# Unused pads in the SBUF pools of a one-core hybrid decoder layer: other starting bytes for weight and moving tiles

## The chip, the cores and the metric

The kernel runs on one core of one Trainium2 chip. The metric is the device time of one execution in microseconds. Before the change it was 1142.21 us, the median of 3 runs (1141.86 to 1142.72).

## What is computed

One decoder layer on 512 tokens of width 1024, in float32. Cut to its products:

```python
h = x
h = h + 0.5 * swiglu(rmsnorm(h), ffn1_w_gate, ffn1_w_up, ffn1_w_down)     # width 2816
u, v, z, xbc, dt = split(rmsnorm(h) @ w_in)
ya = rmsnorm(spatial_gating(gelu(u), layernorm(gelu(v))))                  # 8 heads, chunks of 128
yb = mamba2_mixer(z, xbc, dt)                                              # chunked scan, 16 heads
h = h + concatenate([ya, yb]) @ w_out
h = h + 0.5 * swiglu(rmsnorm(h), ffn2_w_gate, ffn2_w_up, ffn2_w_down)
h = h + sigmoid(rmsnorm(h) @ ple_w_gate + ple_b_gate) * (p @ ple_w_proj)
return rmsnorm(h)
```

## The kernel before

All activations lie with features on the 128 partitions and the 512 tokens along the free dimension. Every large product is done in three passes over float32r parts: a float32 matrix is split into a high part (a cast on ScalarE) and a low part (the rest, a subtraction on VectorE), and TensorE adds high x high, high x low and low x high. `passes` (lines 192 to 196) does this for most products, with 512 moving columns per matmul: the down projections of both FFNs, the input and output projections of the mixer, the final gate. The last three tiles of that gate run in halves of 256 columns.

The up and gate projections of the two FFNs go through `Group.product` (lines 499 to 513), which uses a seven-product scheme over 2 x 2 blocks with 256 moving columns per matmul; line 510 issues these. Here the stationary operand is a 128 x 128 piece of a weight part and the moving one is a piece of an activation form.

The order of work is written out by hand: `run` (line 328) walks a list of steps, loading six steps ahead, splitting two steps ahead, and recording the order of TensorE, VectorE, ScalarE and SyncE as written.

The names that matter here:

- `raw`, `rawb`, `raw0`, `rawd`, `s1`: weights as loaded, 128 x 1024. `whi`, `wlo` and, in the FFNs, for every fourth weight unit `whix`, `wlox`: their parts. TensorE takes 128-column pieces of them as stationary operand.
- `xfa`, `xfb`: activation forms of the FFNs, the moving operands of line 510.
- `ghi`, `glo`: the gated hidden activations, the moving operands of the down projections. `ya`, `yb`: outputs of the two mixers, moving operands of the output projection.
- `x`: normed activations for the input projections and the gate, moving operand there. In one product (the v part, lines 1053 to 1058) the roles are exchanged: `x` is stationary and the weights `whi`, `wlo` move.

SBUF tiles come from three pools. `base` (named `sb`) holds what lives through the program, among it `raw`, `whi` and `wlo`. Two further regions, one growing from the left behind `base` and one that ends at the top of SBUF, are released and opened again between stages: `ffn1_left`, `mix_left`, `ffn2_left` and `ple_left`, `ffn1_right`, `mix_right`, `ffn2_right` and `ple_right`. `REGION` (line 53) says which tile lies where. `open_region` (lines 85 to 89) releases the pool of a side and opens the next:

```python
def open_region(side, name):
    if region[side] is not None:
        region[side].release()
    names[side] = name
    region[side] = tc.alloc_tile_pool(name=name, bufs=1, side=side, reuse_waits="tile")
```

Within a pool, tiles lie one behind the other in the order of their tags. Pieces that TensorE takes from a tile begin 512 bytes, or a multiple of that, behind the tile's start, so a piece begins at the same byte of a 512-byte line as its tile.

Of the kernel before, what the change touches and what calls it, by code (L numbers as in the profile page):

```python
# [22 lines left out]
F32 = mybir.dt.float32  # L23
# [4 lines left out]
P = 128  # L28
# [24 lines left out]
REGION = dict.fromkeys(("raw0", "D1", "X12", "F", "xfa", "xfb", "x", "xs", "u", "emb"), "left") | dict.fromkeys(  # L53
    ("rawb", "whix", "wlox", "s1", "rawd", "ghi", "glo", "g", "u2", "p7", "ya", "yb", "convin", "o"), "right",
)
HEADS = 16
HD = 64
GROUPS = 2
# [18 lines left out]
def layer_kernel(ctx: ExitStack, tc: tile.TileContext, a: dict, out: bass.AP):  # L77
    nc = tc.nc
    PSUM = bass.MemoryType.PSUM
    base = ctx.enter_context(tc.tile_pool(name="sb", bufs=1))  # L80

    region = {"left": None, "right": None}
    names = {}

    def open_region(side, name):
        if region[side] is not None:
            region[side].release()
        names[side] = name
        region[side] = tc.alloc_tile_pool(name=name, bufs=1, side=side, reuse_waits="tile")

    psum = ctx.enter_context(tc.tile_pool(name="ps", bufs=1, space=PSUM))
    dram = ctx.enter_context(tc.tile_pool(name="dr", bufs=1, space=bass.MemoryType.DRAM))
    count = [0]

    def sb(tag, shape=(P, T), dt=F32):
        count[0] += 1
        pool = region[REGION[tag]] if tag in REGION else base
        return pool.tile(list(shape), dt, tag=tag, bufs=BUFS.get(tag, 1), name=f"{tag}_{count[0]}")

    open_region("left", "ffn1_left")  # L100
    open_region("right", "ffn1_right")

    def bank(tag, n):
# [13 lines left out]
    def tmp():  # L117
        return sb("tmp")
# [209 lines left out]
    def run(steps, opened=None):  # L328
# [11 lines left out]
        for i in range(-3, n + 2):  # L340
            if 0 <= i < n - LOADS:
                ahead = i + LOADS
                if opened is not None and i <= opened < ahead and steps[ahead].from_right:
                    held.append(ahead)
                else:
                    do(ahead, "load")
            do(i, "product")
            if i == opened:
                open_region("right", "ffn2_right")
                for k in held:  # L350
                    do(k, "load")
            late = 0 <= i - 1 < n and not steps[i - 1].urgent
            if 0 <= i - 2 < n and len(steps[i - 2].after) > 1:
                steps[i - 2].after[1]()
            for what in ("split", "after") if late else ("after", "split"):
                if what == "split":
                    do(i + 2, "split")
                    do(i + 3, "sums")
                elif 0 <= i - 1 < n and steps[i - 1].after:
                    steps[i - 1].after[0]()  # L360
                if what == "after":
                    do(i, "rest")
# [364 lines left out]
        return Step(product, load, None, split, (out,), True)  # L727

    h = [sb("h") for _ in range(ND)]
    norm = Norm(nc.vector)  # L730
    x_ffn1, x_mix = [], []
    ffn1 = former("ffn1_norm", x_ffn1)
# [32 lines left out]
    def project(unit, w=None):  # L765
# [4 lines left out]

    small = lambda tag: sb(tag, (P, HEADS * NC))

# [4 lines left out]
    nc.vector.tensor_tensor(  # L777
        both[:, :, HEADS : 2 * HEADS],
        w_dt.raw.rearrange("p (k m) -> p k m", k=ND)[:, :, :HEADS],
        both[:, :, :HEADS].bitcast(F32), ALU.subtract,  # L780
    )
# [6 lines left out]
    dt_raw = tmp()  # L788
    nc.vector.tensor_copy(dt_raw[: 2 * HEADS], ps[: 2 * HEADS])

# [24 lines left out]
    for c in range(NC):  # L815
        nc.tensor.transpose(
            dt_ps[:, 2 * c * HEADS : 2 * (c + 1) * HEADS],
            dt_raw[: 2 * HEADS, c * P : (c + 1) * P], ident[: 2 * HEADS, : 2 * HEADS],
# [464 lines left out]
    rows_out(halves[0], r_a)  # L1283
    rows_out(halves[1], factors(halves[1], sq_b))
    for side in region:
        region[side].release()


def _laid_out(i):
# [87 lines left out]
```

## Time and profile before

| | |
|---|---|
| median of 3 runs | 1142.21 us |
| the profiled execution | 1142.69 us |
| its span, first to last instruction | 1141.0 us |
| granted TensorE clock, mean | 0.988 |
| TensorE, matmuls | 1104.4 us busy, 6778 records |
| TensorE, weight loads | 978.6 us busy, 6778 records |
| VectorE / ScalarE / GpSimd | 827.0 / 515.6 / 156.0 us busy |
| moved by DMA | 154.34 MB, 135 GB/s over the span |

In the rows of the profile PE is TensorE with its matmuls, PEld its weight loads, DVE VectorE, ACT ScalarE and POOL GpSimd. A row of groups reads: line, engine, operation, output <- inputs, rows and columns of the array, output shape, count | busy us, mean ns of one | idle us before them and what ended it. A buffer's number is left out of its name, and of two inputs of a matmul the first named is not always the moving one. Matmuls overlap: one starts well before the last has ended, and the ends are modelled. A row of windows reads: stretch, its length, busy us and (count) of the engine, granted clock, DMA share, GB/s.

### The profile page before, as it was taken

The numbers are of one execution on the slowest core, as the hardware profiler recorded it, in microseconds if no ns is written. First come the engines' busy times: TensorE is split into PE (matmuls) and PEld (weight loads), VectorE is DVE, ScalarE is ACT, GpSimd is POOL, SyncE is SP. The second block draws the span as 40 slices with busy tenths as digits, with TensorE's granted clock in tenths as the row PEclk, the third lists the DMA queues.
The fourth block names the chain that finished last, engine by engine and source line by source line (L and its number), as shares of the span: only waits on it lengthen the run. The fifth ranks groups of instructions, "written<-read, shape, count | busy, mean of one in ns | idle before, by whom it ended". The sixth has DMA issues, their size and how long they took to land. (4 is left out here: it accounts for less than half of the span.)

```text
span 1141.0 us, 16731 instructions
## 1 busy us (share of the span) xinstructions
PE 1104.4 (97%) x6778; PEld 978.6 (86%) x6778; DVE 827.0 (72%) x1088; ACT 515.6 (45%) x680; POOL 156.0 (14%) x138
## 2 busy tenths in 40 slices
PE   6899999999999999999999999989999999999997
PEld 5889999999998788777778877888999999999886
DVE  6787767676777687798775564878777677776855
ACT  5644443444344465423543343544434434344555
POOL 1000000000000301476421100000000000000211
PEclk8899999999999999999999999999999999999998
DMA  9566556555621322353422223586666555542512
GB/s 343 140 185 180 159 161 165 136 138 153 185 92 57 93 82 87 98 170 120 130 74 92 76 91 111 139 212 166 167 167 166 153 151 160 144 115 75 166 38 74
DMA packets 46861, 154.34 MB, mean 135 GB/s; under 512 B 5312, under 2 KB 5568, under 8 KB 46784
## 3 DMA queue, kind: packets, MB, share of 16 engines
q1 hardware_dynamic: 34128, 117.98, 31.0%
q0 software_dynamic: 6912, 25.17, 12.5%
q10 hardware_dynamic: 5744, 10.12, 2.8%
q8 instruction: 53, 0.87, 0.3%
q14 instruction: 24, 0.20, 0.1%
HBM read 148.99 MB, written 4.26 MB: 134 GB/s over the span
## 5 line engine op out<-in xcount | busy, mean ns | idle before, releaser
L510 PE MATMUL mm<-xfb,whi 128*128 128x256 f32 x800 | 145.8, 283 | 3.0 <-ACT acc L575 1.9
L510 PEld LDWEIGHTS mm<-xfb,whi 128*128 128x128 f32 x800 | 125.1, 190 | 4.7 <-ACT acc L575 2.1
L510 PE MATMUL mm<-xfb,wlo 128*128 128x256 f32 x400 | 113.2, 283 | 0.1
L397 DVE TENSOR_TENSOR wlo<-raw,whi 128x1024 fp32r<-128x1024 f32 x69 | 84.4, 1223 | 35.9 <-ACT whi L396 35.6
L196 PE MATMUL sm<-ghi,wlo 128*128 128x512 f32 x268 | 105.8, 395 | 0.7 <-DVE wlo L397 0.7
L195 PE MATMUL sm<-glo,whi 128*128 128x512 f32 x268 | 105.1, 392 | 0.1
L194 PE MATMUL sm<-ghi,whi 128*128 128x512 f32 x268 | 104.5, 390 | 0.0
L510 PE MATMUL acc<-xfb,whi 128*128 128x256 f32 x528 | 96.5, 283 | 0.7 <-DVE g L594 0.7
L596 ACT ACTIVATE g<-g 128x512 f32<-128x512 f32 x44 | 27.8, 632 | 143.4 <-DVE g L595 143.4
L396 ACT CAST whi<-raw 128x1024 fp32r<-128x1024 f32 x69 | 71.8, 1046 | 41.0 <-DVE raw L520 16.0
L510 PEld LDWEIGHTS acc<-xfb,whi 128*128 128x128 f32 x528 | 82.8, 190 | 2.2 <-issue 0.9
L510 PE MATMUL acc<-xfb,wlo 128*128 128x256 f32 x264 | 75.0, 284 | 1.5 <-DVE wlo L397 1.5
L510 PEld LDWEIGHTS mm<-xfb,wlo 128*128 128x128 f32 x400 | 76.0, 190 | 0.3 <-DVE wlo L397 0.3
L397 DVE TENSOR_TENSOR wlo<-rawd,whi 128x1024 fp32r<-128x1024 f32 (+1 forms) x37 | 41.5, 1121 | 44.5 <-ACT whi L396 44.4
L525 POOL DMA_DIRECT2D raw<-in_ffn_gu x22 | 18.8, 856 | 395.1 <-DMA raw<-in_ffn_gu 119.2
L649 DVE SCALAR_TENSOR_TENSOR h<-sm,h 128x512 f32<-128x512 f32 x96 | 63.3, 684 | 11.5 <-PE sm L196 11.5
L397 DVE TENSOR_TENSOR wlo<-rawb,whi 128x1024 fp32r<-128x1024 f32 x48 | 58.7, 1224 | 16.7 <-ACT whi L396 16.7
L164 ACT CAST whi<-raw 128x1024 fp32r<-128x1024 f32 x44 | 45.8, 1043 | 48.5 <-issue 14.8
L165 DVE TENSOR_TENSOR wlo<-raw,whi 128x1024 fp32r<-128x1024 f32 x44 | 57.9, 1317 | 12.8 <-ACT whi L164 12.6
L237 POOL TENSOR_TENSOR ssum<-ssum,tmp 128x512 f32<-128x512 f32 x27 | 38.3, 1419 | 207.4 <-ACT tmp L236 206.9
L194 PE MATMUL mm<-x,whi 128*128 128x512 f32 x160 | 64.3, 402 | 0.0
L196 PE MATMUL mm<-x,wlo 128*128 128x512 f32 x160 | 63.4, 396 | 0.0
(332 smaller groups left out, 2969.6 us busy)
## 6 DMA issues: line engine op xcount, KB each, us to landing
raw<-in_ffn_gu SPq DMA_DIRECT2D x56, 512.0 KB, 4.5
rawd<-in_ffn_down SPq DMA_DIRECT2D x40, 512.0 KB, 3.8
rawb<-in_ffn_gu SPq DMA_DIRECT2D x32, 512.0 KB, 4.9
raw<-in_w_in SPq DMA_DIRECT2D x29, 512.0 KB, 3.6
s<-in_ffn_gu SPq DMA_DIRECT2D x22, 512.0 KB, 4.6
raw<-in_ffn_gu POOLq DMA_DIRECT2D x22, 512.0 KB, 5.5
s<-in_ffn_gu POOLq DMA_DIRECT2D x22, 512.0 KB, 7.3
raw<-in_w_out SPq DMA_DIRECT2D x16, 512.0 KB, 3.5
```

Source lines behind the costliest of these rows:

```text
L164: nc.scalar.copy(self.hi[:, c], self.raw[:, c])
L165: nc.vector.tensor_tensor(self.lo[:, c], self.raw[:, c], self.hi[:, c].bitcast(F32), ALU.subtract)
L194: nc.tensor.matmul(ps, whi, xhi, start=first, stop=False)
L195: nc.tensor.matmul(ps, whi, xlo, start=False, stop=False)
L196: nc.tensor.matmul(ps, wlo, xhi, start=False, stop=last)
L237: self.engines[i].tensor_tensor(self.totals[i], self.totals[i], sq, ALU.add)
L396: nc.scalar.copy(self.hi[:, :n], raw[:, :n])
L397: nc.vector.tensor_tensor(self.lo[:, :n], raw[:, :n], self.hi[:, :n].bitcast(F32), ALU.subtract)
L510: nc.tensor.matmul(o, wt[:, c], xt, start=fresh and p == m == n == 0, stop=last and n == 2, skip_group_check=True,)
L525: nc.gpsimd.dma_start(w21.raw, self.src[0], accum_op=ALU.add)
L596: nc.scalar.activation(t, t, AF.Silu)
L649: nc.vector.scalar_tensor_tensor(h[d], ps[d], 0.5, h[d], ALU.mult, ALU.add)
```

## The change

An unused tile of a chosen size, a pad, is put into the pools: 480 bytes per partition into `base` right behind `h`, 480 bytes at the start of `ffn1_left` and `ffn2_left`, 32 bytes at the start of `mix_left` and `ple_left`, and 96 bytes at the end of each pool on the right, which moves the tiles of that side 96 bytes down. `close_region` does the release, and for the right side allots the pad first.

```diff
+PAD = {"sb": 480, "ffn_left": 480, "mix_left": 32, "ple_left": 32, "right": 96}
...
+    count = [0]
+
+    def pad(pool, name):
+        count[0] += 1
+        n = PAD[name.replace("1", "").replace("2", "")]
+        pool.tile([P, n // 4], F32, tag="pad", name=f"pad_{count[0]}")
+
+    def close_region(side):
+        if region[side] is not None:
+
+            if side == "right":
+                pad(region[side], side)
+            region[side].release()
 
     def open_region(side, name):
-        if region[side] is not None:
-            region[side].release()
+        close_region(side)
         names[side] = name
         region[side] = tc.alloc_tile_pool(name=name, bufs=1, side=side, reuse_waits="tile")
+        if side == "left":
+            pad(region[side], name)
...
     h = [sb("h") for _ in range(ND)]
+    pad(base, "sb")
...
     for side in region:
-        region[side].release()
+        close_region(side)
```

No instruction, order or wait differs between the two programs; the tiles' addresses do. Start of a tile within a 512-byte line, in bytes:

| tiles | role on TensorE | before | after |
|---|---|---|---|
| `whi`, `wlo` (and `raw`) | weights; moving in the v part | 416 | 384 |
| `whix`, `wlox` (and `rawb`, `rawd`, `s1`) | weights | 480 | 384 |
| `xfa`, `xfb` (and `raw0`) | moving, 256 columns | 384 | 320 |
| `x` | moving, 512 columns; weights in the v part | 384 | 384 |
| `ghi`, `glo`, `ya`, `yb` | moving, 512 columns | 480 | 384 |
| `h`, `tmp`, `ones`, `onesr` | small products | 384 | 384 |

The pairs that this gives, moving start and weight start:

| products | before | after |
|---|---|---|
| line 510 with `whi`, `wlo` | 384, 416 | 320, 384 |
| line 510 with `whix`, `wlox` | 384, 480 | 320, 384 |
| `ghi`, `glo`, `ya`, `yb` with `whi`, `wlo` | 480, 416 | 384, 384 |
| `ghi`, `glo` with `whix`, `wlox` | 480, 480 | 384, 384 |
| `x` with `whi`, `wlo` | 384, 416 | 384, 384 |
| `whi`, `wlo` moving, `x` as weights | 416, 384 | 384, 384 |

More of the change, by code (lines that the diff above doesn't have):

```diff
@@ L83, in layer_kernel @@
     names = {}
+    count = [0]
[8 more added lines that the diff above has]
+            region[side].release()
     def open_region(side, name):
-        if region[side] is not None:
-            region[side].release()
+        close_region(side)
         names[side] = name
         region[side] = tc.alloc_tile_pool(name=name, bufs=1, side=side, reuse_waits="tile")
+        if side == "left":
+            pad(region[side], name)
     psum = ctx.enter_context(tc.tile_pool(name="ps", bufs=1, space=PSUM))
     dram = ctx.enter_context(tc.tile_pool(name="dr", bufs=1, space=bass.MemoryType.DRAM))
-    count = [0]
     def sb(tag, shape=(P, T), dt=F32):
```

## The prediction

> **What bounds the kernel now.** I read the page first, then the waits of TensorE, then the costliest groups by form, then single stretches. The page's engine line and its slices:
>
> ```profile
> PE 1104.4 (97%) x6778; PEld 978.6 (86%) x6778; DVE 827.0 (72%) x1088; ACT 515.6 (45%) x680; POOL 156.0 (14%) x138
> PE   6899999999999999999999999989999999999997
> PEclk8899999999999999999999999999999999999998
> ```
>
> PE is busy in 97% of the span; after the first two slices hardly anything is left between its instructions, and the clock is granted in full. The other engines have a quarter of their time or more to spare. The waits of PE (engine and line, releaser, us in total, times, longest) agree; the three longest:
>
> ```profile
> PE mm L510 <- ACT rawd L724: 4.4, 1, 4.4
> PE mm L194 <- ACT ghi L711: 2.8, 1, 2.8
> PE mm L510 <- DVE g L594: 2.2, 2, 1.1
> ```
>
> The time is therefore PE's: the number of matmuls times the distance from one start to the next. "Busy" hides that distance, since matmuls overlap: a 512-column one is 390 to 400 ns long and the next starts after some 230. So I look at starts, and at what runs beside them (start us, length us; PEld is the weight load):
>
> ```profile
> 402.16 0.40 PE L196 MATMUL acc<-x,wlo 128*128 128x512 f32 x1
> 402.17 0.19 PEld L194 LDWEIGHTS acc<-x,whi 128*128 128x128 f32 x1
> 402.40 0.40 PE L194 MATMUL acc<-x,whi 128*128 128x512 f32 x1
> ```
>
> Each matmul is accompanied by the load of the next one's weights, which begins with it. Two streams are thus read from SBUF at once, and the change alters where they begin. I call "distance" the start of the weights that are being loaded minus the start of the moving operand, in bytes of a 512-byte line, by the table of starts above.
>
> Do such starts show in the time now? Three stretches of unbroken 512-column matmuls. Each has its first and last row; the windows view then counts the instructions (x) that run within a window set so that the first and the last of them are the outermost.
>
> ```profile
> 181.24 0.39 PE L194 MATMUL sm<-ghi,whix 128*128 128x512 f32 x1
> ...
> 186.47 0.39 PE L196 MATMUL sm<-ghi,wlox 128*128 128x512 f32 x1
> ```
> ```profile
> 705.76 0.39 PE L194 MATMUL acc<-ya,whi 128*128 128x512 f32 x1
> ...
> 732.54 0.39 PE L194 MATMUL mm<-ya,whi 128*128 128x512 f32 x1
> ```
> ```profile
> 401.23 0.40 PE L195 MATMUL acc<-x,whi 128*128 128x512 f32 x1
> ...
> 422.46 0.40 PE L196 MATMUL mm<-x,wlo 128*128 128x512 f32 x1
> ```
> ```profile
> 181.42:186.50 5.08, 5.08 (x24) 1.00 0.91 177
> 706.00:732.60 26.60, 26.60 (x118) 1.00 0.39 105
> 401.40:422.60 21.20, 21.20 (x92) 1.00 0.29 88
> ```
>
> First stretch, moving at 480 and weights at 480 (distance 0): 24 matmuls, so 23 intervals in 5.23 us, 227.4 ns each. Second, 480 and 416 (distance -64): 117 intervals in 26.78 us, 228.9 ns. Third, 384 and 416 (distance +32): 91 intervals in 21.23 us, 233.3 ns. That three places differ could be the stage they lie in, so I ask the groups too:
>
> ```profile
> L194 PE MATMUL sm<-ghi,whix 128*128 128x512 f32 x84 | 32.7, 390 | 0.0
> L195 PE MATMUL sm<-glo,whi 128*128 128x512 f32 x268 | 105.1, 392 | 0.1
> L196 PE MATMUL mm<-ya,wlo 128*128 128x512 f32 x40 | 15.7, 393 | 0.0
> L195 PE MATMUL mm<-yb,whi 128*128 128x512 f32 x40 | 15.6, 390 | 0.0
> L195 PE MATMUL mm<-x,whi 128*128 128x512 f32 x160 | 63.2, 395 | 0.0
> L196 PE MATMUL acc<-x,wlo 128*128 128x512 f32 x104 | 41.3, 397 | 1.6 <-DVE wlo L165 1.6
> L195 PE MATMUL mm<-wlo,x 128*128 128x512 f32 x40 | 15.8, 395 | 0.0
> ```
>
> Mean lengths rise in the same order: 390 at distance 0, 390 to 393 at -64, 395 to 397 at +32, and 395 again where the roles are exchanged (moving whi at 416, weights x at 384, distance -32). The ends are modelled, but over the whole program the lengths tell what the starts of the three stretches tell: some 5 ns from the best pair to the worst.
>
> The 256-column matmuls of L510 come from the chain of waits (start, us, what), where a run of them stands as one piece:
>
> ```profile
> 797.46 2.88 PE mm L510 x24
> 811.63 5.68 PE mm L510 x48
> 822.88 2.85 PE acc L510 x24
> ```
>
> 5.68/48 is 118.3 ns, 2.85/24 is 118.8, and one run takes 2.88/24 = 120.0. Their distances are +32 with whi and +96 with whix; no run stands at 0 or 64.
>
> **The change part by part.** It adds no instruction and no wait: the same instructions stand in the same order on every engine, with the same semaphores, so nothing is queued behind anything new. What changes is where operands begin. After it the pairs are: L510 moving 320, weights 384 (distance +64); every product of L194 to L196 384 and 384 (distance 0). Counts:
>
> ```profile
> 0.00:1141.00 1141.00, 453.08 (x3696) 0.99 0.47 135
> L194 PE MATMUL mm<-x,whi 128*128 128x512 f32 x160 | 64.3, 402 | 0.0
> L194 PE MATMUL acc<-x,whi 128*128 128x512 f32 x104 | 42.0, 404 | 0.0
> L194 PE MATMUL mm<-whi,x 128*128 128x512 f32 x40 | 16.0, 399 | 0.0
> L194 PE MATMUL acc<-whi,x 128*128 128x512 f32 x24 | 9.5, 395 | 0.0
> L194 PE MATMUL acc<-yb,whi 128*128 128x512 f32 x24 | 9.6, 400 | 0.8 <-DVE h L1142 0.8
> L194 PE MATMUL sm<-x,whi 128*128 128x256 f32 x48 | 13.6, 283 | 0.0
> ```
>
> (The first row is the windows view for line L510 alone.) Each product runs three passes, so:
>
> 1. Products with x on either side, 512 columns: 3 x (160 + 104 + 40 + 24) = 984. From ±32 to 0: 233.3 - 227.4 = 5.9 ns each, 5.8 us. If the new pair reaches only the 228.9 of distance -64, 4.3 us.
> 2. ghi, glo, ya, yb with whi: 3 x (268 + 2 x (40 + 24)) = 1188 (ya and yb alike). From -64 to 0: 228.9 - 227.4 = 1.5 ns, 1.8 us. The 3 x 84 with whix stay at distance 0: nothing.
> 3. L510, 3696 matmuls of 256 columns from distance 32 or 96 to 64, a pair that no row shows. Nearest are the 512-column rows, where -64 stands 4.4 ns below ±32, and 0 stands 5.9 below. If the cost grows with the columns streamed, half of 4.4 comes here, 2.2 ns; if it arises only while weights load, which is 0.19 us either way, all of it. I take the middle, 3.3 ns, 12.2 us. Upper bound of the gain: half of 227.4 is 113.7, so 118.3 - 113.7 = 4.6 ns, 17.0 us. Lower bound, a loss: the 120.0 of the one run, 1.7 ns more, 6.3 us.
> 4. The 3 x 48 = 144 with x of 256 columns: the same 3.3 ns, 0.5 us; bounds with term 3.
> 5. VectorE, ScalarE and DMA see new starts too. The same subtraction stands twice with its input at 416 and at 480:
>
> ```profile
> L397 DVE TENSOR_TENSOR wlo<-raw,whi 128x1024 fp32r<-128x1024 f32 x69 | 84.4, 1223 | 35.9 <-ACT whi L396 35.6
> L397 DVE TENSOR_TENSOR wlo<-rawb,whi 128x1024 fp32r<-128x1024 f32 x48 | 58.7, 1224 | 16.7 <-ACT whi L396 16.7
> ```
>
> 1223 against 1224 ns: nothing. Should one grow all the same, PE covers it, as long as it stays within the quarter that DVE has free.
>
> Sum: 5.8 + 1.8 + 12.2 + 0.5 = 20.3 us of PE time. Not all of it reaches the end: PE's 36.6 us outside its busy time do not shrink, and where PE runs ahead it next meets g of L594 and wlo of L397, for which it waits a little already. I keep 17 of 20, some 17.3 us. The profiled execution took 1142.7 us around its span of 1141.0: 1142.7 - 17.3 = 1125.4. The median of the runs shown, 1142.21, lies 0.5 lower, so 1124.9, and I say 1125; the rivals' times below are counted from that median.
>
> A rule speaks against all this. In this trace the spacing of equal matmuls differs by 5.9 ns between pairs of starts. The Trainium skill, page "SBUF — State Buffer", section "Who interferes with whom", gives TensorE two independent read ports, for the moving operand and for weight loads, and says "PE and ACT never wait on anyone"; its "Specifications (TRN2)" name lines of 16 bytes. All starts here, before and after, are multiples of 32 bytes, so by that page the sum would be zero. The trace disagrees about the pairs, though not about who causes it; the rule is the third rival below.
>
> The same skill's page "TensorE: Matmul & The Clock Gate", section "Back-to-back issue gap", gives N/2.4 + 2.5 ns alone, an estimate of 109.2 and 215.8 here; reaching it everywhere would be worth about 71 us. No run here shows that, and it bounds nothing above.
>
> **The rivals.**
>
> First: only the 512-column products gain, because 256 columns last as long as a weight load and the load itself sets 118 ns. For it: three runs above lie within 1.7 ns although their distances differ. Against it: the 120.0 and the 118.3 show that the pair matters there a little. Terms 1 and 2, 7.6 us, at 17 of 20: 1142.2 - 6.5 = 1135.7. Chance 0.19.
>
> Second, slower: not the distance counts but the moving start alone. 480 is the good start and 384 or 416 the bad one; every row above fits that as well, since all the short ones move at 480. Then x keeps its 233.3, and ghi, glo, ya and yb lose what they have: 1188 x (233.3 - 228.9) = 5.2 us and 252 x 5.9 = 1.5 us. L510 at 320 stays at 118.3. 1142.2 + 6.7 = 1148.9. It decides if stretches of ya, now at 384, show over 230 ns. Against it: with the moving start at 480 fixed, weights at 480 and at 416 still differ by 1.5 ns. Chance 0.14.
>
> Third: starts do nothing, and what differs between x and ghi is the stage and the size of the tiles. Time 1142. For it: all x products lie in other stages than the ghi ones. Against it: ya and yb are tiles of 512 columns like x and lie in the same middle part, yet go with ghi. Chance 0.10.
>
> Fourth: the pair 320 and 384 falls into the 120.0 pattern. Terms 1 and 2 are gained and 6.3 us lost: about 1141, within the bound of no change. Chance 0.07.
>
> **How the numbers follow.** The forecast has 0.50. Its own range comes from term 3 and 4: with all of 4.6 ns and nothing lost on the way, 25.3 us, 1117; with 2.2 ns and 17 of 20, 13.6 us, 1129. The range from 1116 to 1146 holds the forecast, the first, third and fourth rival, 0.86, less the tails around them; the second lies outside. A measurement of this kernel can tell about 0.2% from no change, 2.3 us. Faster by more: 0.50 + 0.19 = 0.69. Within: 0.10 + 0.07 = 0.17. Slower: 0.14.
>
> **What would show it.** Right: 24 matmuls of L510 in 2.75 to 2.80 us in the chain (now 2.85), the x stretch below 229 ns and mean lengths of the x groups near 390, VectorE's 1223 unchanged. The first rival shows x at 390 with L510 still at 2.84; the second shows ya at 395; the third leaves all groups as they are; the fourth shows 2.88 throughout. The forecast is wrong if L510 does not shorten, whatever x does, and also if PE shortens as said but its waits for DVE and ACT grow by as much.

## The result, and the profile after

The changed kernel takes 1135.33 us, the median of 5 runs (1134.26 to 1138.19), beside 1142.21 for the kernel before in 5 runs of the same chip. The ratio is 0.994, 95% interval 0.9923 to 0.9957: faster by 6.9 us, where 17 were forecast. The profiled execution took 1135.33 us around a span of 1133.6. Lines are 16 or 17 higher than before: L510 is now L526, L194 to L196 are L210 to L212, L397 is L413. In the kernels of the experiments they shift a little further.

The page's engine line, its slices and the three longest waits of PE, after the change:

```profile
PE 1093.3 (96%) x6778; PEld 974.3 (86%) x6778; DVE 827.7 (73%) x1088; ACT 515.4 (45%) x680; POOL 156.6 (14%) x138
PE   6899999999999999999999999989999999999997
PEclk9899999999999999999999999999999999999999
```
```profile
PE mm L526 <- ACT rawd L740: 5.2, 1, 5.2
PE acc L526 <- DVE g L610: 3.1, 2, 1.7
PE mm L210 <- ACT ghi L727: 2.6, 1, 2.6
```

PE lost 11.1 us of busy time and its weight loads 4.3, the other engines none; the picture is otherwise the same. Two stretches of 512 columns, ya and x, and one of 256 columns with x, each with its first and last row and its count:

```profile
700.78 0.39 PE L210 MATMUL acc<-ya,whi 128*128 128x512 f32 x1
...
727.30 0.39 PE L210 MATMUL mm<-ya,whi 128*128 128x512 f32 x1
```
```profile
1086.16 0.39 PE L210 MATMUL acc<-x,whi 128*128 128x512 f32 x1
...
1102.26 0.39 PE L212 MATMUL mm<-x,wlo 128*128 128x512 f32 x1
```
```profile
1102.60 0.28 PE L211 MATMUL sm<-x,whi 128*128 128x256 f32 x1
...
1116.76 0.28 PE L212 MATMUL sm<-x,wlo 128*128 128x256 f32 x1
```
```profile
701.00:727.40 26.40, 26.40 (x118) 1.00 0.40 108
1086.40:1102.30 15.90, 15.90 (x72) 1.00 0.12 34
1102.89:1116.80 13.91, 13.91 (x118) 1.00 0.00 1
```

ya: 117 intervals in 26.52 us, 226.7 ns, where 228.9 stood. x: 71 in 16.10 us, 226.8, where x stood at 233.3. This stretch of x lies in the last gate; the stretch of the mixer that was shown of before is 227.3 ns now (97 matmuls, 96 intervals in 21.82 us). The 256 columns: the third window begins after the matmul of 1102.60 has ended, so 118 intervals in 14.16 us, 120.0 ns. They got longer. The groups (lengths):

```profile
L211 PE MATMUL sm<-glo,whi 128*128 128x512 f32 x268 | 104.5, 390 | 0.2 <-DVE glo L631 0.2
L211 PE MATMUL mm<-x,whi 128*128 128x512 f32 x160 | 62.4, 390 | 0.0
L210 PE MATMUL sm<-ghi,whix 128*128 128x512 f32 x84 | 32.8, 390 | 0.0
L212 PE MATMUL mm<-ya,wlo 128*128 128x512 f32 x40 | 15.6, 389 | 0.0
L211 PE MATMUL mm<-wlo,x 128*128 128x512 f32 x40 | 15.6, 389 | 0.0
L413 DVE TENSOR_TENSOR wlo<-raw,whi 128x1024 fp32r<-128x1024 f32 x69 | 84.4, 1223 | 35.9 <-ACT whi L412 35.6
```

The groups of 512 columns shown here now have one length, 389 or 390, whatever the stage; those compared of before ranged from 390 to 397. Groups that hold some long matmuls behind a wait or a break still lie higher, the first pass of x at 397 where it was 402. VectorE's subtraction is where it was. What did not come is seen in the chain, runs of L526:

```profile
792.01 2.83 PE mm L526 x24
806.04 5.65 PE mm L526 x48
```

2.83/24 is 117.9 ns, 5.65/48 is 117.7, where 118.8 and 118.3 stood: 0.6 to 1 ns instead of 3.3.

Not all that PE saved reached the end. The first 50 us, in which the clock is still rising, are set apart by the windows; before, then after:

```profile
0.00:50.00 50.00, 37.26 (x177) 31.94 (x178) 35.18 (x58) 32.90 (x54) 7.03 (x15) 0.82 0.79 266
```
```profile
0.00:50.00 50.00, 36.30 (x173) 31.00 (x174) 35.29 (x58) 32.94 (x54) 7.08 (x15) 0.91 0.79 266
```

From there on PE is busy 1104.4 - 37.3 = 1067.1 us before and 1057.0 after, 10.1 less; the span shrinks by 7.4. So 2.7 us turned into time in which PE does not work. PE's waits from there on tell the same: those of more than 0.15 us add up to 16.4 us before and 19.1 after.

### The profile page after: what moved, and what is told of

Read it like the earlier page. It is cut to its first block, busy times and chain, and to the rows that moved or that the text cites. A ratio compares the mean times of both kernels' runs of the same rounds, so it can differ in the third digit from the quotient of the medians.

```text
span 1133.6 us, 16731 instructions
## 1 busy us (share of the span) xinstructions
PE 1093.3 (96%) x6778; PEld 974.3 (86%) x6778; DVE 827.7 (73%) x1088; ACT 515.4 (45%) x680; POOL 156.6 (14%) x138
## 5 line engine op out<-in xcount | busy, mean ns | idle before, releaser
L526 PE MATMUL mm<-xfb,whi 128*128 128x256 f32 x800 | 144.9, 283 | 3.6 <-ACT acc L591 2.5
L526 PEld LDWEIGHTS mm<-xfb,whi 128*128 128x128 f32 x800 | 124.4, 190 | 5.2 <-ACT acc L591 2.7
L526 PE MATMUL mm<-xfb,wlo 128*128 128x256 f32 x400 | 113.0, 283 | 0.1
L413 DVE TENSOR_TENSOR wlo<-raw,whi 128x1024 fp32r<-128x1024 f32 x69 | 84.4, 1223 | 35.9 <-ACT whi L412 35.6
L212 PE MATMUL sm<-ghi,wlo 128*128 128x512 f32 x268 | 105.0, 392 | 1.1 <-DVE wlo L413 1.0
L210 PE MATMUL sm<-ghi,whi 128*128 128x512 f32 x268 | 104.5, 390 | 0.0
L526 PE MATMUL acc<-xfb,whi 128*128 128x256 f32 x528 | 96.4, 284 | 1.4 <-DVE g L610 1.4
L526 PEld LDWEIGHTS acc<-xfb,whi 128*128 128x128 f32 x528 | 82.8, 191 | 2.7 <-issue 1.5
L526 PEld LDWEIGHTS mm<-xfb,wlo 128*128 128x128 f32 x400 | 77.3, 193 | 0.3 <-DVE wlo L413 0.3
L526 PE MATMUL acc<-xfb,wlo 128*128 128x256 f32 x264 | 75.0, 284 | 1.4 <-DVE wlo L413 1.4
L413 DVE TENSOR_TENSOR wlo<-rawd,whi 128x1024 fp32r<-128x1024 f32 (+1 forms) x37 | 41.5, 1121 | 44.4 <-ACT whi L412 44.4
L413 DVE TENSOR_TENSOR wlo<-rawb,whi 128x1024 fp32r<-128x1024 f32 x48 | 58.8, 1224 | 16.6 <-ACT whi L412 16.6
L210 PE MATMUL mm<-x,whi 128*128 128x512 f32 x160 | 63.5, 397 | 0.0
L212 PE MATMUL mm<-x,wlo 128*128 128x512 f32 x160 | 62.5, 390 | 0.0
```

Source lines behind the costliest of these rows:

```text
L210: nc.tensor.matmul(ps, whi, xhi, start=first, stop=False)
L212: nc.tensor.matmul(ps, wlo, xhi, start=False, stop=last)
L413: nc.vector.tensor_tensor(self.lo[:, :n], raw[:, :n], self.hi[:, :n].bitcast(F32), ALU.subtract)
L526: nc.tensor.matmul(o, wt[:, c], xt, start=fresh and p == m == n == 0, stop=last and n == 2, skip_group_check=True,)
```

## The experiments

Eight further kernels were run; at the end the change and one of them were run once more, side by side. All but "x alone" start from the changed kernel, and most differ from it only in the sizes of pads, which are given for each region apart there (`ffn1_left`, `ffn2_left` and so on). The two kernels with other widths or half weight loads leave out or add work, so their times (1239.49 and 1125.94 us, one run each) tell nothing of the change, and their spacings alone are read. Spacings are means of start to start in unbroken runs of the trace.

**Everything 32 bytes further**

```diff
-PAD = {"sb": 480, ... "right": 96}
+PAD = {"sb": 512, ... "right": 64}
```

> The changed kernel with every operand of TensorE's large products 32 bytes further: moving 416 with weights 416 (distance 0) for all 512-column products, moving 352 with weights 416 (distance 64) for the 256-column ones of the FFNs. Theory 'distance': the spacing is set by weight start minus moving start alone, so nothing moves: 226.7 ns for 512 columns, 117.8 for the FFNs' 256, 120.0 for the 256-column ones of the last gate at distance 0, about 1135 us. Rival 'moving start': 480 and 384 are good, 416 is bad as it was in the kernel before (233.3 with weights at 384), so 512 columns go back to some 233 ns, 2400 x 6 = 14 us more, 1149. Rival 'multiples of 64': both operands at a multiple of 64 bytes are what helped; at 352 and 416 neither is, so some 229 to 233 ns, 1140 to 1149.

1136.2 us in its one run, beside 1143.66 for the kernel before. A group with x moving from 416, and the chain:

```profile
L212 PE MATMUL mm<-x,whi 128*128 128x512 f32 x160 | 62.3, 389 | 0.0
```
```profile
960.42 5.65 PE mm L527 x48
```

389 and 117.7: nothing moved, though 416 as a moving start gave 395 before. With both starts moved alike the distance stays and so does the spacing; both rivals fall.

**Two scans of the distance**

```diff
-"ffn1_left": 480, "ffn2_left": 480, "mix_left": 32, "ple_left": 32, "mix_right": 96
+"ffn1_left": 352, "ffn2_left": 224, "mix_left": 480, "ple_left": 416, "mix_right": 192   # first scan
+"ffn1_left": 96, "ffn2_left": 32, "mix_left": 288, "ple_left": 160, "mix_right": 0       # second scan
+XFB = {"ffn1_left": 64, "ffn2_left": 64}   # first: a further pad ahead of xfb; second: 64 and 32
```

> The changed kernel with other pads on the left and in the mixer's right pool, so that several distances (weight start minus moving start) can be read from one profile: 256 columns at 192 (xfa, first FFN), 128 (xfb, first FFN), -192 (xfa, second FFN), 256 (xfb, second FFN); 512 columns at 64 (x in the mixer), 128 (x in the last gate), 96 (ya and yb), 0 (ghi, glo, unchanged). Theory 'parity': all multiples of 64 are alike, 117 to 118 ns and 226 to 229 ns, and only odd multiples of 32 (here 96) are dear, 233. Rival 'size of the distance': the cost grows with the distance, so that 64 shows 229 and 128 over 231 for 512 columns, and 128 to 256 over 119 for 256 columns. Rival 'load bound': 256 columns stay between 117 and 120 at every distance, since something other than the pair sets them.

> As the scan before with other distances: 256 columns at -64 (xfa, first FFN), -128 (xfb, first FFN), 0 (xfa, second FFN), -32 (xfb, second FFN); 512 columns at 256 (x in the mixer), -128 (x in the last gate), -96 (ya and yb). Theory 'parity': multiples of 64 show 117 to 118 and 226 to 229 ns; -32 shows 118.3 and -96 shows 233. At 0, 256 columns show 120.0 as they did in the last gate of the changed kernel. Rival 'size of the distance': 256 is the dearest of all, over 233 for 512 columns. Rival 'load bound': 256 columns stay between 117 and 120 at each.

The kernels took 1147.32 and 1141.73 us in one run each. Groups with x at distance 64 (first scan) and 256 (second), and ya at 96 (first):

```profile
L213 PE MATMUL mm<-x,whi 128*128 128x512 f32 x160 | 63.2, 395 | 0.0
...
L213 PE MATMUL mm<-ya,whi 128*128 128x512 f32 x40 | 15.9, 396 | 0.0
```
```profile
L213 PE MATMUL mm<-x,whi 128*128 128x512 f32 x160 | 62.5, 390 | 0.0
```

The chain of the first scan in its second FFN, where xfb stands at 256 and xfa at -192:

```profile
987.86 2.74 PE acc L533 x24
...
998.92 2.88 PE acc L533 x24
1001.80 5.60 PE mm L533 x48
```

2.88/24 is 120.0 at distance 256. The 2.74 us are a step of xfa, 114.2 ns; its first matmuls are still longer. The pair of steps in 5.60 us holds one of xfb, so the other, of xfa, took 2.72, 113.3 ns, which the starts in the trace show too once such a step has settled. All values together, with those of the two kernels; a distance and the same plus 256 are in one row:

| distance | 256 columns, ns | 512 columns, ns |
|---|---|---|
| 0 or 256 | 120.0 (all three places) | 226.7 (both) |
| 32 | 118.3 | 233.3 |
| 64 or -192 | 117.8, some runs 113.3 (at -192 in the first scan, most) | 233.3 |
| 96 | 118.7, some runs 120.0 | 234.1 |
| 128 or -128 | 118.5 to 120.0 | 232.4 |
| 160 or -96 | 120.0 | 233.3 |
| 192 or -64 | 117.8 | 228.9 |
| 224 or -32 | 116.7 | 233.3 |

The 232.4 is the last gate's long stretch, 71 intervals in 16.50 us. "Parity" falls: 64 is as dear as 32 for 512 columns, and 128 nearly so. "Size of the distance" falls: 256 is as good as 0. "Load bound" said 117 to 120 at every distance: most rows fit, but 116.7 and above all 113.3 lie below. The row of 64 is the one that matters for the forecast: 512 columns gain nothing there.

**Other widths at distance 64**

```diff
...
+    if names["left"] == "ffn2_left":
+        xhi = xlo = xf.wide(i)                      # 384 columns of the same form
+    else:
+        xhi, xlo = xhi[:, :192], xlo[:, :192]
...
```

> The changed kernel with other widths at distance 64: in the first FFN each matmul of the seven-product scheme streams 192 moving columns instead of 256, in the second 384 (part of the products is left out in the first and other columns are added in the second, and each fresh bank is filled by one more matmul of 512 columns). Theory 'load bound': a matmul cannot start before the next weights are in, which takes some 118 ns, so 192 columns stay at 115 to 118 ns, and 384 columns show 160 ns of streaming plus 11 to 15, 171 to 175. Rival 'fixed addition': the spacing is the streaming time plus 11 to 13 ns at any width, so 192 columns show 80 + 12 = 92 ns, and the first FFN's matmuls save 26 ns each, over 1800 of them some 47 us.

One step of 192 columns in the first FFN, with its count, and the chain with 384 in the second:

```profile
110.17 0.39 PE L541 MATMUL acc<-xfb,whi 128*128 128x192 f32 x2
...
112.74 0.28 PE L541 MATMUL acc<-xfb,wlo 128*128 128x192 f32 x1
```
```profile
110.35:112.80 2.45, 2.45 (x24) 1.00 0.46 40
```
```profile
887.52 4.24 PE mm L541 x24
```

23 intervals in 2.57 us are 111.7 ns at 192 columns, and 4.24/24 is 176.7 at 384, over the 171 to 175 expected. 192 columns do not fall to 92: something near 111 ns holds them. That is below the 115 to 118 that "load bound" gave, and 117.8 lies above it, so whether 256 columns are held by the same thing is left open by this run.

**Half a weight load**

```diff
-    c = slice((2 * p + m) * P, (2 * p + m + 1) * P)
-    o = ps[:, m * HT : (m + 1) * HT]
+    c = slice((2 * p + m) * P, (2 * p + m) * P + 64)
+    o = ps[:64, m * HT : m * HT + n_cols]           # 256 in the first FFN, 192 in the second
```

> The changed kernel (distance 64) with weight pieces of 64 columns instead of 128 in the seven-product scheme, so that half of each product's output is left out and each weight load has half the columns; 256 moving columns in the first FFN, 192 in the second (where a part of the tokens is left out as well); each fresh bank is filled by one more matmul of 512 columns. Theory 'load bound': the load of the next weights sets the 111 ns that 192 columns took and leaves 256 columns hardly any room; with half the load 192 columns fall to 80 ns and an addition of 5 to 15, 85 to 95, and 256 columns to 107 plus 3 to 8, 110 to 115. Rival 'pair': what is over the streaming time comes from the two streams meeting, whichever is longer, so 256 columns stay at 117 to 118 and 192 columns keep some 111.

A weight load of the change and one of this kernel, a step of 256 columns in the first FFN, then the chain with 192 in the second:

```profile
L526 PEld LDWEIGHTS mm<-xfb,whi 128*128 128x128 f32 x800 | 124.4, 190 | 5.2 <-ACT acc L591 2.7 <-issue 1.3
...
L533 PEld LDWEIGHTS mm<-xfb,whi 128*64 128x64 f32 x800 | 97.3, 136 | 5.7 <-ACT acc L598 2.0
```
```profile
159.02 0.40 PE L533 MATMUL mm<-xfb,whi 128*64 128x256 f32 x2
...
161.75 0.28 PE L533 MATMUL mm<-xfb,wlo 128*64 128x256 f32 x1
```
```profile
159.20:161.80 2.60, 2.60 (x24) 1.00 0.00 0
```
```profile
993.48 2.17 PE acc L533 x24
```

The load is shorter, 136 ns instead of 190. 192 columns fall to 2.17/24 = 90.4 ns: there the load was the bound. 256 columns take 23 intervals in 2.73 us, 118.7 ns, no less than with the whole load. At 256 columns the length of the load is not what sets 118; each theory is right at one width.

**x alone, from the kernel before**

```diff
+    if name in ("mix_left", "ple_left"):
+        region[side].tile([P, 8], F32, tag="pad", name=f"pad_{name}")
```

> The kernel before with one part of the change: 32 bytes of pad at the start of the left pools of the mixer and of the last gate, so that x begins at 416, where its weights begin already (distance 0); all other starts stay as before. Theory 'distance': the 984 products of 512 columns with x go from 233.3 to some 227 ns, 6 us less, the 144 of 256 columns go from 118.4 to 120.0, 0.2 us more. If seven tenths of what PE saves reach the end, as in the change itself, the time falls by 4 us to some 1138; if all of it does, by 5.8. Rival 'moving start': x at 416 is as bad a start as the weights were when they moved from 416 in the kernel before, so it stays at 233 ns and the time at 1142.

1139.04 us (5 runs) beside 1142.75 (9 runs), ratio 0.9968 (0.9956 to 0.9981). x, and a group that was not touched:

```profile
L197 PE MATMUL mm<-x,whi 128*128 128x512 f32 x160 | 62.3, 390 | 0.0
...
L198 PE MATMUL mm<-ya,wlo 128*128 128x512 f32 x40 | 15.7, 393 | 0.0
```

The x products went to 390, ya stayed at 393, and the time fell by 3.7 us. So x carries about half of the change's gain; "moving start" falls a second time, on timed runs.

**The FFNs at other distances**

```diff
-"ffn1_left": 480, "ffn2_left": 480
+"ffn1_left": 64, "ffn2_left": 64          # distance -32
+"ffn1_left": 224, "ffn2_left": 384        # distances -192 and 160
```

> The changed kernel with the 256-column products of both FFNs at distance -32 instead of 64 (pads of 64 bytes instead of 480 at the start of the FFNs' left pools). Theory 'distance': the scan showed 117.0 ns for the larger part of them at -32 in the second FFN, the change shows 117.5, so 3696 x 0.5 = 1.8 us less PE time and 1 to 2 us less time than the change, 1133 to 1134. Rival: the 117.0 belonged to the neighbourhood of the other half of that FFN, which stood at distance 0, and not to the pair; then it falls back to 117.8 or over, and the time is that of the change or above, 1135 to 1137.

> The changed kernel with the 256-column products of the first FFN all at distance -192 and those of the second all at 160; 512 columns as in the change. Theory 'period of 256 bytes': the scans gave the same value at 0 and 256, at 128 and -128, and at 192 and -64, so -192 must behave as 64 does in the change, 117.5 ns in the mean with most runs at 117.8, and 160 as -96, of which there is only a 512-column value. Rival 'no period': -192 is a pair of its own and locks to the 113.3 ns that most runs of xfa showed in the first scan, and the first FFN is 1800 x 4 = 7 us shorter, a kernel of some 1128 us even with 160 at 118 ns.

The chain at -32, then that of the second kernel, in its second FFN at 160 and a step of its first FFN at -192 (24 matmuls):

```profile
987.46 5.60 PE mm L527 x48
```
```profile
992.91 5.76 PE mm L527 x48
```
```profile
89.59 0.40 PE L527 MATMUL mm<-xfb,whix 128*128 128x256 f32 x2
...
92.30 0.28 PE L527 MATMUL mm<-xfb,wlox 128*128 128x256 f32 x1
```

-32 gives 5.60/48 = 116.7 ns throughout and 1133.62 us (5 runs), ratio 0.9921 (0.9908 to 0.9935). 160 gives 120.0. At -192 the step shown has 23 intervals in 2.71 us, 117.8; so had most steps of the first FFN, with some at 113.3, as at 64 in the change: the period of 256 bytes holds, and the many steps at 113.3 in the first scan were not the pair's own. That kernel took 1138.61 us in one run.

Where they came from, the starts in the traces of the two scans suggest: a step's spacing goes with what ran just before it. In the second FFN of the first scan all 18 steps of xfa (-192) that begin right behind a step of xfb at 256, at 120.0 ns, settle at 113.3; of the other four, which begin behind 512-column products, two do. In the second scan it is the other way round: of the steps of xfb (-32) right behind xfa at distance 0, ten of eleven settle at 117.8, and behind other products, nearly all of 512 columns, 19 of 20 settle at 116.7. No kernel here varied the neighbour alone.

**The change and the distance -32, side by side**

> The changed kernel as it is, on the same chip and beside the same runs of the kernel before as the next one. If its first measurement holds, the ratio is 0.992 to 0.996, some 1135 us, and seven tenths of the 10.8 us that its matmuls' spacing lost.

> The changed kernel with the FFNs' 256-column products at distance -32, once more and beside the change. Theory 'distance': 117.5 to 116.7 ns on 3696 matmuls is 2.9 us of PE time, so 1 to 3 us below the change, a ratio of 0.990 to 0.993. Rival: PE's waits give it back, the same time as the change.

For the change: 1135.21 us (5 runs), ratio 0.9932 (0.9919 to 0.9946). With -32: 1133.17 us (4 runs), ratio 0.9917 (0.9903 to 0.993), both beside 1142.9 for the kernel before. The medians differ by 2.0 us as worked out and in the same direction as the first time (1133.62 and 1135.33), and every run with -32 (1133.03 to 1133.66) lies below every run of the change (1134.04 to 1136.05), but the two intervals of the ratios overlap. It is the fastest version measured, by a little.

## Why the prediction was wrong in size

**What bounds the kernel** was read rightly: PE's spacing, changed by the distance between the starts of two streams. The shift by 32 bytes and x alone show that it is the distance and no single start.

**Term 1**, x to distance 0, was right: 5.9 ns were forecast; 233.3 to 226.8 is 6.5 in the last gate, 233.3 to 227.3 is 6.0 in the mixer. **Term 2**, ghi, glo, ya and yb, was right: 1.5 ns forecast, 2.2 measured in ya. **Term 5**, nothing on VectorE, was right: 1223 ns as before.

**Term 3 failed**, and with it the forecast. It took for the new pair at 64 that "nearest are the 512-column rows, where -64 stands 4.4 ns below ±32". It treated 64 as if it were -64. They are different places in a period of 256 bytes: at -64 512 columns take 228.9, at 64 they take 233.3, as at 32. The source of the 3.3 ns was not there. Measured are 0.6 to 1 ns, 2 to 4 us instead of 12.2. The other half of the step, to price 256 columns by rows of 512, failed as well: at -64 itself 256 columns hold 117.8, 0.5 ns below the 118.3 of distance 32, where 2.2 to 4.4 were expected, and at 0, where 512 columns are cheapest, 256 are at their dearest, 120.0. The upper bound of 113.7 was not out of reach, though: the steps that settle at 113.3 have that spacing at this very pair, but in the change they are 10 of some 130. **Term 4**, priced like term 3, had the wrong sign: the 144 products of 256 columns with x went to 120.0, 0.2 us more instead of 0.5 less.

The terms add up. Over all starts of the two traces that follow without a break, the mean fell by 5.6 ns for x, by 1.9 for ghi, glo, ya and yb with whi, and by 1.0 for L510: 5.5 + 2.3 + 3.5 - 0.2 = 11.1 us, which is what PE lost.

**What reaches the end** was put at 17 of 20. It was 7.4 of 10.1 in the profile. The rest went into PE's waits, as the prediction had said, only more of it. Of the three shown above that for g alone lies behind the first 50 us: with its other line it grew from 4.2 to 5.3 us, 1.1 of the 2.7. The remainder is spread over growths of some tenths of a us in waits for wlo and others, most of them on VectorE.

**The first rival** named the time, 1135.7, and what would be seen, x at 390 and L510 little moved. Part of that is luck: L510 did gain some 3.5 us, and PE's time outside its busy time grew by about as much, from 36.6 to 40.3 us. Its reason, that the weight load itself sets 118 ns, is right at 192 columns only: there half a load took 111 to 90. At 256 columns half a load left 118.7. So its number came out for a reason that does not hold. **The second rival** had the moving start decide; two kernels refute it. **The third** had starts do nothing; the groups refute it. **The fourth** had a pattern of 120.0 for 64; no step of the change took it on L510. It is real, but it is the pattern of distance 0 and 256; at 96 and 128 some steps have it.

A word on the rule that spoke against the change. Kernels that differ in nothing but pads differ by some 7 ns a matmul (ya: 234.1 at distance 96, 226.7 at 0). The Trainium skill's page "SBUF — State Buffer", section "Who interferes with whom", says that TensorE never waits on anyone; for its own two streams the traces here disagree. The Trainium skill's page "TensorE: Matmul & The Clock Gate", section "LDWEIGHTS (loading the stationary operand)", gives P/1.2 ns for a load of P columns, an estimate of 107 ns for 128. The 111.7 of 192 moving columns lies just above it, and the records of a whole and of half a load, 190 and 136 ns, differ by 54 ns for 64 columns, which agrees.

What stays open: on what the two streams meet with a period of 256 bytes, and how the pattern of a step hangs on the one before it. Were every matmul of L510 at 113.3 instead of 117.5 ns, PE would save 15.5 us more, an estimate from these rows; no kernel here tried for it. Starts between the multiples of 32 bytes were not tried.

## What to carry to other kernels

Where TensorE is busy throughout, look at the starts of its matmuls, not at their lengths or the busy share: equal matmuls with different spacing point to where their operands begin. A pad can change that spacing by 3% and costs no instruction, only some bytes of SBUF in each partition, but the best distance depends on the moving width (0 for 512 columns, -32 for 256 here), so each width is scanned; several distances fit into one kernel if each stage gets its own. Do not carry a value from one distance to its mirror image, nor from one width to another.

## What the runs showed of the hardware that was not expected

- The spacing depends on the distance between weights and moving operand with a period of 256 bytes: 0 and 256, 64 and -192, 128 and -128 agree at both widths, where both were measured.
- At distance 0, 256 columns take 120.0 and 512 take 226.7: 106.7 ns for 256 columns more, and 13.3 ns on top at either width. At 64 the addition grows with the width: taking 106.7 ns for 256 columns, 11 ns at 256, 16.7 at 384 and 20 at 512 (117.8, 176.7 and 233.3 measured).
- A long run of equal matmuls settles into a fixed pattern: 226.7 or 120.0 ns each at distance 0, and at 64 or -192 either 117.8 on the mean or 113.3, kept for the rest of the step. Which of the two goes with what ran just before: in the first scan, of the steps at -192 right behind a step at 120.0, 18 of 18 took 113.3.
- With 192 moving columns, a weight load of 128 columns holds the spacing at 111.7 ns, and one of 64 columns lets it fall to 90.4.
